# High weights against both parts of an activation in one 512-column matmul

## The chip, the core and the metric

The kernel runs on one core of one Trainium2 chip. The metric is device time in microseconds, the median of three timed runs. TensorE (PE in the profile) does the matmuls, with its weight loads listed apart as PEld; VectorE is DVE, ScalarE is ACT, GpSimd is POOL and SyncE is SP, which here issues the weight transfers.

## What is computed

Five blocks follow one another on 256 tokens (272 in the first part, with 16 meta tokens ahead) of 2048 features, all in float32:

```python
h = h + mla_mixer(rms_norm(h))        # 272 tokens
h = h + swiglu(rms_norm(h))           # first feed-forward, 272 tokens
h = h + rglru_mixer(rms_norm(h))      # recurrent mixer
h = h + swiglu(rms_norm(h))           # second feed-forward
h = rms_norm(h)[:, N_META:]           # 256 tokens
for layer in range(2):                # second block: four attentions, gate, output projection
    x = x + einsum(y * silu(gate), w_out[layer])

def swiglu(h, w_gu, w_down):
    g, u = split(h @ w_gu, 2)
    return (silu(g) * u) @ w_down     # 2048 -> 2 x 5632 -> 2048

def rglru_mixer(h, w_in, ...):
    xb, yb = split(h @ w_in, 2)       # 2048 -> 2 x 2048
    yb = gelu(yb)
    xb = conv(xb); r, i = gates(xb)   # two 128x128 gate matrices for each of 16 blocks
    hs = scan(a(r), b(i, xb))
    return (hs * yb) @ w_o
```

## The kernel before

Features lie on the 128 partitions and tokens on the free axis, so a gemm makes one tile of 128 output features by 256 or 272 tokens. Every float32 number is split into a high and a low part of type float32r, `xh` and `xl` for an activation, `wh` and `wl` for a weight, and a product is three matmuls for each 128 features of the contraction (`mm3`, L224 to L226): `wh` with `xh`, `wh` with `xl`, `wl` with `xh`. All three add into the same PSUM tile `p`. A first or second feed-forward `gu` gemm has 16 such steps, a `dn` (down) gemm 11, an `lru_in` gemm 16 and an `lru_o` gemm 8.

Weights come from HBM in pieces of up to 1024 columns (`wblock`): SP loads `wraw` (4 buffers), ACT casts it into `wh` (L212, 6 buffers), DVE subtracts into `wl` (L187, 5 buffers). There are four PSUM tiles `p`.

The feed-forward (`ffn`) has four chunks of 11 hidden tiles. For each hidden tile f, `gu` runs two gemms (gate and up), DVE multiplies each by the norm's factor (L478, L480), ACT takes silu, DVE multiplies, and the product is split (`hid`). Then 16 `dn` gemms, one for each tile m of h, are added to h by DVE (L497). One hidden tile of the next chunk is made ahead of the `dn` gemms, except in the last chunk. In the last chunk of the second feed-forward, each finished tile of h goes through the final norm's tile work: squares on ACT and POOL, a scale on DVE (L936), and a split (L251, L252).

The recurrent mixer (`lru`) goes over 16 blocks n, in groups of four. Each has a 272-column gemm for `xb`, a convolution on DVE (L524), a split `xch`, `xcl`, two gates `pg` (three matmuls each), and a 256-column gemm for `yb`. After four blocks the scan is done on DVE (L570). Then two passes of 16 gemms over `lru_o`, added to h by DVE (L582).

The second block (`block2`) runs 32 rounds of a pair of heads with gemms of q, k and gate, attention, and output projections.

The order in which each engine takes its instructions is set at build time by a scheduler that orders the traced program by its own estimate of times. A tile has to wait until a buffer of its pool is free. Before, the high and low parts are separate slots of the pool `s` of 66; the small pools `a`, `w`, `r`, `b` hold 10, 11, 3 and 5.

Of the kernel before, what the change touches and what calls it, by code (L numbers as in the profile page):

```python
# [9 lines left out]
F32 = mybir.dt.float32  # L10
# [5 lines left out]
D = 2048  # L16
# [27 lines left out]

SLOTS = {"s": 66, "a": 10, "w": 11, "r": 3, "b": 5}
WB = (4, 6, 5)
# [13 lines left out]


class Lazy:
    """Traced at its first use, so that it queues behind what is traced before."""

# [10 lines left out]
class Net:  # L75
# [48 lines left out]
    def use_log_exp(self, after=None):  # L124
        """One table set for exp and ln; the next logarithm is queued behind its load."""
        if after is None:
            self.log_exp = self.nc.scalar.preload_act_table_set("natural_log_exp_and_others")
        else:
            with self.tc.issue_after(after.ins):
                self.log_exp = self.nc.scalar.preload_act_table_set("natural_log_exp_and_others")  # L130
# [14 lines left out]
    def zeropad(self, n):  # L145
        """Pairs of [128, 256] operands whose first half stays zero."""
        self.zp = []
        self.zpi = 0
        for _ in range(n):
            pr = (self.slot("zph", F32R), self.slot("zpl", F32R))  # L150
            for t in pr:
                self.nc.gpsimd.memset(t[:, 0:128].bitcast(F32), 0.0)
            self.zp.append(pr)

    def split_zp(self, x):
        """split(x) into columns 128..255 of a zero-padded pair."""
        h, l = self.zp[self.zpi % len(self.zp)]
        self.zpi += 1
        self.nc.scalar.copy(h[:, 128:256], x)
        self.sub(l[:, 128:256], x, h[:, 128:256])  # L160
        return h, l

    def stackpad(self, n):
        """Tiles of three bands of 16 rows, with zeros between them."""
        self.st3 = [self.slot("st3", F32R) for _ in range(n)]
        self.st3i = 0
        for t in self.st3:
            self.nc.gpsimd.memset(t[0:96].bitcast(F32), 0.0)

    def stack3(self, x, n, order):  # L170
        """High, high and low part of 16 rows (by order: high first, low last) as bands of one contraction."""
        t = self.st3[self.st3i % len(self.st3)]
        self.st3i += 1
        b = [t[32 * i:32 * i + 16, 0:n] for i in order]
        self.nc.scalar.copy(b[0], x)
        self.nc.scalar.copy(b[1], x)
        self.sub(b[2], x, b[0])
        return t
# [9 lines left out]

    def split(self, x, name, n, p=slice(0, 128), tag="s"):
        nc = self.nc  # L190
        h = self.slot(name + "h", F32R, tag=tag)
        l = self.slot(name + "l", F32R, tag=tag)
        nc.scalar.copy(h[p, 0:n], x)
        self.sub(l[p, 0:n], x, h[p, 0:n])
        return h, l
# [6 lines left out]
    def wblock(self, ap, n, wp=1024, raws=None):  # L202
        """Loads n columns in pieces of wp and splits each into its two float32r parts."""
        nc = self.nc
# [23 lines left out]
    def gemm(self, p, w, xs, sl, off=0):  # L228
        n = len(xs)
        for k, (xh, xl) in enumerate(xs):  # L230
            self.mm3(p, self.wcol(w, off + k * 128, 128), (xh[:, sl], xl[:, sl]), k == 0, k == n - 1)

    def rsqrt(self, name, ms, n, scale=1.0, eps=EPS):
        """scale / sqrt(ms + eps): exp(-ln/2) and one Newton step."""
        nc = self.nc
# [10 lines left out]
    def norm_tile(self, st, m, src, gcol, sl, n, sq=True):  # L246
        """One feature tile on its way into a norm: split(src*g) and the running sum of squares."""
        nc = self.nc
        xh = self.slot("xh", F32R)
        xl = self.slot("xl", F32R)  # L250
        self.last_norm = nc.scalar.activation(xh[:, 0:n], src, AF.Copy, scale=gcol)  # L251
        nc.vector.scalar_tensor_tensor(xl[:, 0:n], src, gcol, xh[:, 0:n].bitcast(F32), ALU.mult, ALU.subtract)  # L252
        st.setdefault("x", []).append((xh, xl))
        if sq:
            self.sumsq(st, src, n)
# [20 lines left out]

# [1 line left out]
    def mla(self, st, nxt):  # L278
# [13 lines left out]
        for i in (4, 5, 6, 7, 0, 1, 2, 3, 8):  # L292
# [9 lines left out]
            if i == 5:  # L302
                with self.tc.issue_after(self.last_norm.ins):
# [7 lines left out]
                    st["accs"] = [sq[0][:, j * T:j * T + T] for j in range(4)]  # L311
                c = self.slot("craw")
                nc.vector.tensor_tensor(c, p4, rb(), ALU.mult)
                self.sumsq(skv_st, c, T)
                ckv_raw.append(c)
            c = self.slot("craw")
            nc.vector.tensor_tensor(c, p, rb(), ALU.mult)
# [72 lines left out]
    def split_stacked(self, x, name, n):  # L390
        """Of each half (one head) of x, both parts in one tile: the high one in its own half, the low one in the other."""
        out = []
# [19 lines left out]
    def softmax(self, s, n, rows, mask):  # L412
        """exp(s + mask - max) / sum over the free axis; kept negated up to the exponential."""
        nc = self.nc
# [44 lines left out]

# [1 line left out]
    def ffn(self, l, st, t0, after):  # L461
        """after(m): what follows on the finished tile m of h."""
        nc, a = self.nc, self.a
# [6 lines left out]
        def gu(f):  # L470
            w = self.wblock(a[f"gu{l}"][f], 2048)
            pg = self.ps()[:, 0:n]
            self.gemm(pg, w, X, sl)
            w = self.wblock(a[f"gu{l}"][FF + f], 2048)
            pu = self.ps()[:, 0:n]
            self.gemm(pu, w, X, sl)
            g = self.tmp("g")[:, sl]
# [8 lines left out]
        for c in range(C):  # L486
# [5 lines left out]
            for m in range(KD):  # L492
                w = self.wblock(a[f"dn{l}"][c, m], FCH * 128)
                p = self.ps()[:, 0:n]
                self.gemm(p, w, H[c * FCH:(c + 1) * FCH], sl)
                hm = self.h[m][:, t0:T]
                nc.vector.tensor_tensor(hm, hm, p, ALU.add)  # L497
                if c == C - 1:
                    after(m)

# [1 line left out]
    def lru(self, st, nxt):  # L502
# [7 lines left out]
        for n0 in range(0, KD, 4):  # L510
            la, th = self.big("la"), self.big("th")
            IX, YB = [], []
            for i in range(4):
# [31 lines left out]
                w = self.wblock(a["lru_in"][16 + n], 2048)  # L545
                p = self.ps()[:, 0:SEQ]
                self.gemm(p, w, X, slice(NM, T))
                if i % 2 == 0:
# [25 lines left out]
        for c in range(2):  # L574
            for mb in range(8):
                w = self.wblock(a["lru_o"][c, mb], 2048)
                for m2 in range(2):
                    m = mb * 2 + m2
                    p = self.ps()[:, 0:SEQ]
                    self.gemm(p, w, Y[c * 8:c * 8 + 8], sl, m2 * 1024)  # L580
                    hm = self.h[m][:, NM:T]
                    nc.vector.tensor_tensor(hm, hm, p, ALU.add)  # L582
                    if c == 1:
                        self.norm_tile(nxt, m, hm, self.col("norm_ffn1", m), sl, SEQ)

    def lru_coef(self):
        """-8*softplus(-lambda) on [128, 16]."""
        nc = self.nc
# [17 lines left out]

# [1 line left out]
    def block2(self, l, st, rb, first_done, after):  # L608
# [6 lines left out]
        def forget(ft):  # L615
            """Running sum of softplus(-(f + bias)) as one row per head."""
            p = self.psh.tile([128, 512], F32, tag="h", name="fT")
# [15 lines left out]
        def values(mx, hf):  # L633
# [5 lines left out]
            for tt in range(2):  # L639
# [8 lines left out]
                p = p[:, sl]  # L648
                vh = self.slot("vh", F32R)[:, sl]
                vl = self.slot("vl", F32R)[:, sl]  # L650
                rc = rcol()[:, tt:tt + 1]
# [78 lines left out]
    def softplus(self, z, rows, n, tag="w"):  # L730
        """max(z, 0) + log(1 + exp(-|z|))"""
        nc = self.nc
# [46 lines left out]
    def diagpad(self, n):  # L779
        """Pairs of [128, 256] operands, zero off the two diagonal blocks (one per head)."""  # L780
        self.dp = []
        self.dpi = 0
        for _ in range(n):
            pr = (self.slot("dph", F32R), self.slot("dpl", F32R))
            for t in pr:
# [4 lines left out]
    def diag(self, x, c):  # L790
        """The two heads of x (its columns c) as the blocks of a diagonal pair."""
        pr = self.dp[self.dpi % len(self.dp)]
# [7 lines left out]
    def soft(self, q, k, masks, NC, i):  # L800
        """Transposed weights of a pair of heads: of keys 0..127, and of keys 128..255 for queries 128..255."""
        nc = self.nc
# [93 lines left out]
    def rcols(self, rb):  # L896
        """Per-token factors as columns: the diagonal blocks of the broadcast rows."""
        nc = self.nc
# [7 lines left out]

# [1 line left out]
    def all(self):  # L908
# [19 lines left out]
    def second(self, st):  # L928
# [13 lines left out]
        def factors():  # L942
            """The two norms in a row: 1 / sqrt(ms + eps), and 1 / sqrt(ms2 / (ms + eps) + eps) times it."""
            ms, ms2 = self.pa("ms")[:, sl], self.pa("ms2")[:, sl]
# [29 lines left out]

# [1 line left out]
def _tiles(w):  # L976
    """[K, M] -> [M/128, 128 (k), K/128 * 128 (m)]"""
    k, m = w.shape
# [4 lines left out]
def _cols(v):  # L983
    """[n*128] -> [128, n]"""
    return np.asarray(v).reshape(-1, 128).T
# [43 lines left out]
def _arrays(inp):  # L1029
# [48 lines left out]
    def kchunks(w, kc, mpb):  # L1078
        """[K, D] -> [K/(kc*128), D/(128*mpb), 128, mpb*kc*128]"""
        k, d = w.shape  # L1080
# [38 lines left out]
```

## Time and profile before

| what | us |
|---|---|
| median of 3 runs (3217.25 to 3219.3) | 3217.95 |
| span of the profiled execution | 3216.7 |
| PE busy | 3187.9 |
| DVE busy | 2162.1 |
| ACT busy | 1755.1 |
| POOL busy | 606.6 |

The span runs from the first to the last instruction of one profiled execution; it lies 1.25 us under the median. Busy times overlap between engines. A matmul's own duration (some 280 ns for 256 columns) contains the time through the pipeline, so what a matmul costs in a stream is the distance from its start to the start of the next one.

### The profile page before, as it was taken

How to read it: one execution, taken by the hardware profiler on the slowest of the kernel's cores; microseconds unless marked ns; L12 is line 12 of the kernel's file. 1: busy time of each engine (PE TensorE's matmuls, PEld its weight loads, DVE VectorE, ACT ScalarE, POOL GpSimd, SP SyncE). 2: the span in 40 equal slices, each digit the busy share in tenths (PEclk: the TensorE clock that was granted, in tenths of full speed). 3: DMA queues.
4: the chain of work that ended last, by engine and by line, in shares of the span. 5: the costliest groups of instructions: out<-in, count | busy, mean ns of one | idle time of the engine just before them, and what ended most of it. 6: DMA issues, size and time to landing. Idle time of an engine off the chain costs nothing.

```text
span 3216.7 us, 64486 instructions
## 1 busy us (share of the span) xinstructions
PE 3187.9 (99%) x25996; PEld 3154.1 (98%) x25996; DVE 2162.1 (67%) x3672; ACT 1755.1 (55%) x2971; POOL 606.6 (19%) x743
## 2 busy tenths in 40 slices
PE   8999999999999999999999999999999999999999
PEld 8998999999999999999999999999999999999999
DVE  7777655555555678865555555568788778778876
ACT  6655533434444576754444444456677666667764
POOL 2000100000000134310000000023244463144453
PEclk9999999999999999999999999999999999999999
DMA  6343556556565555566565656656555545555554
GB/s 215 113 122 111 173 165 187 176 160 190 161 193 173 165 185 175 161 194 186 169 202 172 202 180 186 190 166 200 165 166 170 169 151 174 158 174 168 170 161 131
DMA packets 164862, 549.43 MB, mean 171 GB/s; under 512 B 18753, under 2 KB 37441, under 8 KB 164561
## 3 DMA queue, kind: packets, MB, share of 16 engines
q1 hardware_dynamic: 162720, 540.49, 54.5%
q0 software_dynamic: 1840, 4.82, 0.5%
q8 instruction: 203, 3.33, 0.4%
q14 instruction: 99, 0.80, 0.1%
HBM read 543.13 MB, written 2.10 MB: 170 GB/s over the span
## 4 chain that ended last, share of the span: by engine, by line
PE 92%; DVE 3%; ACT 2%; issue 2%; POOL 1%; DMA 0%; SPq 0%; POOLq 0%; DVEq 0%; ACTq 0%
PE p L224 29%; PE p L225 29%; PE p L226 29%; DVE wl L187 1%; ACT wh L212 1%; PE o L225 1%; PE o L224 0%; PE o L226 0%; DVE xl L252 0%; PE s L224 0%; PE s L225 0%; PE s L226 0%; PE s L438 0%; DVE hs L570 0%; POOL gwl L531 0%
## 5 line engine op out<-in xcount | busy, mean ns | idle before, releaser
L212 ACT CAST wh<-wraw 128x1024 fp32r<-128x1024 f32 (+2 forms) x1108 | 1086.8, 982 | 1003.4 <-PE p L225 777.9
L187 DVE TENSOR_TENSOR wl<-wraw,wh 128x1024 fp32r<-128x1024 f32 (+2 forms) x1108 | 1293.2, 1168 | 334.0 <-issue 248.9
L224 PE MATMUL p<-xh,wh 128*128 128x256 f32 (+1 forms) x5104 | 1451.9, 284 | 7.9 <-ACT wh L212 6.7
L225 PE MATMUL p<-xl,wh 128*128 128x256 f32 (+1 forms) x5104 | 1452.1, 285 | 1.0 <-DVE xl L252 1.0
L226 PE MATMUL p<-xh,wl 128*128 128x256 f32 (+1 forms) x5104 | 1450.1, 284 | 0.3 <-DVE wl L187 0.2
L224 PEld LDWEIGHTS p<-xh,wh 128*128 128x128 f32 x5104 | 963.6, 189 | 10.4 <-ACT wh L212 6.7
L225 PEld LDWEIGHTS p<-xl,wh 128*128 128x128 f32 x5104 | 963.6, 189 | 5.0 <-DVE xl L252 2.4
L226 PEld LDWEIGHTS p<-xh,wl 128*128 128x128 f32 x5104 | 963.3, 189 | 1.9 <-DVE wl L187 1.0
L225 PE MATMUL p<-hidl,wh 128*128 128x272 f32 (+1 forms) x1408 | 400.2, 284 | 0.0
L226 PE MATMUL p<-hidh,wl 128*128 128x272 f32 (+1 forms) x1408 | 400.1, 284 | 0.0
L224 PE MATMUL p<-hidh,wh 128*128 128x272 f32 (+1 forms) x1408 | 399.9, 284 | 0.0
L226 PEld LDWEIGHTS p<-hidh,wl 128*128 128x128 f32 x1408 | 265.2, 188 | 0.0
L225 PEld LDWEIGHTS p<-hidl,wh 128*128 128x128 f32 x1408 | 265.1, 188 | 0.0
L224 PEld LDWEIGHTS p<-hidh,wh 128*128 128x128 f32 x1408 | 265.1, 188 | 0.0
L265 POOL TENSOR_TENSOR acc<-acc,sq 128x256 f32<-128x256 f32 (+1 forms) x81 | 76.3, 942 | 989.8 <-ACT sq L264 909.1
L224 PE MATMUL p<-yh,wh 128*128 128x256 f32 x768 | 216.6, 283 | 0.0
L225 PE MATMUL p<-yl,wh 128*128 128x256 f32 x768 | 216.0, 282 | 0.0
L226 PE MATMUL p<-yh,wl 128*128 128x256 f32 x768 | 215.9, 281 | 0.0
L265 POOL TENSOR_TENSOR accf<-accf,sq 128x256 f32<-128x256 f32 x15 | 15.4, 1026 | 706.2 <-ACT sq L264 706.2
L225 PEld LDWEIGHTS p<-yl,wh 128*128 128x128 f32 x768 | 145.0, 189 | 0.6 <-issue 0.5
L224 PEld LDWEIGHTS p<-yh,wh 128*128 128x128 f32 x768 | 144.6, 189 | 0.9 <-DVE h L704 0.5
L226 PEld LDWEIGHTS p<-yh,wl 128*128 128x128 f32 x768 | 145.0, 189 | 0.1
(352 smaller groups left out, 4269.5 us busy)
## 6 DMA issues: line engine op xcount, KB each, us to landing
wraw<-gu SPq DMA_DIRECT2D x352, 512.0 KB, 4.3
wraw<-dn SPq DMA_DIRECT2D x128, 512.0 KB, 3.5
wraw<-in SPq DMA_DIRECT2D x128, 512.0 KB, 4.3
wraw<-lru_in SPq DMA_DIRECT2D x64, 512.0 KB, 4.1
wraw<-g SPq DMA_DIRECT2D x64, 512.0 KB, 3.8
wraw<-out SPq DMA_DIRECT2D x64, 512.0 KB, 3.7
wraw<-v SPq DMA_DIRECT2D x56, 512.0 KB, 4.1
wraw<-dn SPq DMA_DIRECT2D x128, 192.0 KB, 2.6
```

Of the source, the lines that this page charges most:

```text
L187: return self.nc.vector.tensor_tensor(out, x, h.bitcast(F32), ALU.subtract)
L212: nc.scalar.copy(h[:, 0:c], raw)
L224: nc.tensor.matmul(p, lh, rh, start=first, stop=False)
L225: nc.tensor.matmul(p, lh, rl, start=False, stop=False)
L226: nc.tensor.matmul(p, ll, rh, start=False, stop=last)
L265: (eng or nc.gpsimd).tensor_tensor(st[key], st[key], s[:, 0:n], ALU.add)
```

## The change

For gemms of 256 tokens in the second feed-forward (`gu` and `dn`) and in the recurrent mixer (the `yb` half of `lru_in`, and `lru_o`), the three matmuls of a contraction step become two (`gemm2`): `wh` against `xh` and `xl` side by side, 512 columns into the two halves of a PSUM tile, and `wl` against `xh`, 256 columns into the first half. So the two halves of the PSUM tile have to be added. Where the gemm ends in a residual add (`gemm_add`), DVE adds the halves to h one after the other. Elsewhere (`gemm_any`) ACT copies the second half into a tile `sum`, and DVE adds the first half to it; what follows then reads `sum` in place of `p`. For 272 tokens nothing changes in the matmuls, since two parts would be 544 columns.

To stand side by side, the two parts of an activation are now one tile `Pair` of 2 x 272 columns. They have a pool `x` of 27 pairs, and the pool `s` of single tiles falls from 66 to 12. The tile `craw` of the first mixer moves to the pool `b`. All splits use the pairs, in the parts of the kernel whose matmuls stay the same too.

```diff
-SLOTS = {"s": 66, "a": 10, "w": 11, "r": 3, "b": 5}
+SLOTS = {"x": 27, "s": 12, "a": 10, "w": 11, "r": 3, "b": 5}
...
+    def pair(self, name, n=T):
+        t = self.slots["x"].tile([128, 2 * T], F32R, tag="x", name=name)
+        p = Pair((t[:, 0:n], t[:, T:T + n]))
+        p.both = t.rearrange("p (j c) -> p j c", c=T)[:, :, 0:n]
+        return p
...
+    def gemm2(self, p, w, xs, sl, off=0):
+
+        n = len(xs)
+        for k, x in enumerate(xs):
+            wh, wl = self.wcol(w, off + k * 128, 128)
+            self.nc.tensor.matmul(halves(p, SEQ), wh, x.both[:, :, sl], start=k == 0, stop=False)
+            self.nc.tensor.matmul(p[:, 0:SEQ], wl, x[0][:, sl], start=False, stop=k == n - 1)
+
+    def gemm_any(self, w, xs, sl, off=0):
+
+        p = self.ps()
+        n = sl.stop - sl.start
+        if n > SEQ:
+            p = p[:, 0:n]
+            self.gemm(p, w, xs, sl, off)
+            return p
+        self.gemm2(p, w, xs, sl, off)
+        t = self.tmp("sum")[:, 0:SEQ]
+        self.nc.scalar.copy(t, p[:, SEQ:512])
+        self.nc.vector.tensor_tensor(t, p[:, 0:SEQ], t, ALU.add)
+        return t
+
+    def gemm_add(self, hm, w, xs, sl, off=0):
+
+        p = self.ps()
+        n = sl.stop - sl.start
+        if n > SEQ:
+            self.gemm(p[:, 0:n], w, xs, sl, off)
+            self.nc.vector.tensor_tensor(hm, hm, p[:, 0:n], ALU.add)
+            return
+        self.gemm2(p, w, xs, sl, off)
+        for j in range(2):
+            self.nc.vector.tensor_tensor(hm, hm, p[:, j * SEQ:j * SEQ + SEQ], ALU.add)
...
             w = self.wblock(a[f"gu{l}"][f], 2048)
-            pg = self.ps()[:, 0:n]
-            self.gemm(pg, w, X, sl)
+            pg = self.gemm_any(w, X, sl)
...
                 w = self.wblock(a[f"dn{l}"][c, m], FCH * 128)
-                p = self.ps()[:, 0:n]
-                self.gemm(p, w, H[c * FCH:(c + 1) * FCH], sl)
-                hm = self.h[m][:, t0:T]
-                nc.vector.tensor_tensor(hm, hm, p, ALU.add)
+                self.gemm_add(self.h[m][:, t0:T], w, H[c * FCH:(c + 1) * FCH], sl)
...
-                p = self.ps()[:, 0:SEQ]
-                self.gemm(p, w, X, slice(NM, T))
+                p = self.gemm_any(w, X, slice(NM, T))
...
-                    p = self.ps()[:, 0:SEQ]
-                    self.gemm(p, w, Y[c * 8:c * 8 + 8], sl, m2 * 1024)
                     hm = self.h[m][:, NM:T]
-                    nc.vector.tensor_tensor(hm, hm, p, ALU.add)
+                    self.gemm_add(hm, w, Y[c * 8:c * 8 + 8], sl, m2 * 1024)
```

**On PE, in a `gu` gemm of the second feed-forward.** Two contraction steps of one gemm before (out<-moving,weights and the moving columns):

```order
L224 MATMUL p_25154<-xh_16911,wh_25144 128x256
L225 MATMUL p_25154<-xl_16912,wh_25144 128x256
L226 MATMUL p_25154<-xh_16911,wl_25145 128x256
L224 MATMUL p_25154<-xh_16956,wh_25144 128x256
L225 MATMUL p_25154<-xl_16957,wh_25144 128x256
```

and three steps of such a gemm with the change:

```order
L255 MATMUL p_22954<-x_16411,wh_22944 128x512
L256 MATMUL p_22954<-x_16411,wl_22945 128x256
L255 MATMUL p_22954<-x_16448,wh_22944 128x512
L256 MATMUL p_22954<-x_16448,wl_22945 128x256
L255 MATMUL p_22954<-x_16473,wh_22944 128x512
```

Nothing moved between the steps; L224 and L225 became one instruction.

**On DVE, in the last chunk of the second feed-forward**, one period between two `dn` gemms before, where `h` is the residual and `p` the gemm's PSUM tile:

```order
L497 TENSOR_TENSOR h_93<-h_93,p_26128 128x256
L187 TENSOR_TENSOR wl_26293<-wraw_26290,wh_26292 128x1024
L936 TENSOR_SCALAR h_93<-h_93,cols_83 128x256
L252 SCALAR_TENSOR_TENSOR xl_26168<-h_93,cols_83,xh_26167 128x256
L187 TENSOR_TENSOR wl_26299<-wraw_26296,wh_26298 128x384
L497 TENSOR_TENSOR h_93<-h_93,p_26186 128x256
```

and with the change:

```order
L282 TENSOR_TENSOR h_93<-h_93,p_23737 128x256
L193 TENSOR_TENSOR wl_23869<-wraw_23866,wh_23868 128x1024
L303 SCALAR_TENSOR_TENSOR x_23672<-h_93,cols_83,x_23672 128x256
L282 TENSOR_TENSOR h_93<-h_93,p_23737 128x256
L978 TENSOR_SCALAR h_93<-h_93,cols_83 128x256
L193 TENSOR_TENSOR wl_23875<-wraw_23872,wh_23874 128x384
L282 TENSOR_TENSOR h_93<-h_93,p_23784 128x256
```

The second add stands four places behind the first, and the subtraction for the norm (L252, now L303) now belongs to the tile before and has moved ahead of the scale (L936, now L978).

**On ACT, in the recurrent mixer**, at the last block of a group of four, before (`gate` reads a gate's PSUM tile `pg`; `gel` is the gelu of `yb`):

```order
L212 CAST wh_14419<-wraw_14417 128x1024
L553 ACTIVATE gel_14195<-yb_14032 128x256
L556 ACTIVATE gel_14195<-gel_14195 128x256
L538 ACTIVATE gate_14122<-pg_14118,cols_83 128x272
L538 ACTIVATE gate_14128<-pg_14124,cols_83 128x272
L212 CAST wh_14506<-wraw_14504 128x1024
L544 ACTIVATE th_13513<-la_13512 128x272
```

and with the change:

```order
L229 CAST wh_14294<-wraw_14292 128x1024
L584 ACTIVATE gate_13934<-pg_13930,cols_83 128x272
L268 COPY sum_13990<-p_13957 128x256
L584 ACTIVATE gate_13940<-pg_13936,cols_83 128x272
L590 ACTIVATE th_13364<-la_13363 128x272
L229 CAST wh_14343<-wraw_14341 128x1024
```

The copy of the `yb` gemm's second half stands between the two gates, and the gelu of that block has moved behind them.

## Rows read from the trace of the kernel before

**Rows 1.** The page, its first part: busy us, share of span, instructions.

```profile
PE 3187.9 (99%) x25996; PEld 3154.1 (98%) x25996; DVE 2162.1 (67%) x3672; ACT 1755.1 (55%) x2971; POOL 606.6 (19%) x743
```

**Rows 2.** The page, the chain that ended last, by engine.

```profile
PE 92%; DVE 3%; ACT 2%; issue 2%; POOL 1%; DMA 0%; SPq 0%; POOLq 0%; DVEq 0%; ACTq 0%
```

**Rows 3.** Windows, inside both feed-forwards: stretch, its us, busy us per engine.

```profile
core 0: us, PE busy (x) PEld busy (x) DVE busy (x) ACT busy (x) POOL busy (x), PEclk, DMA share, GB/s
350.00:1130.00 780.00, 780.00 (x6229) 780.00 (x6228) 421.93 (x552) 325.12 (x417) 10.31 (x13) 1.00 0.58 175
1450.00:2180.00 730.00, 730.00 (x6170) 730.00 (x6169) 416.47 (x557) 322.05 (x425) 26.48 (x25) 1.00 0.60 184
```

**Rows 4.** Timeline of PE, second block: first and last of 32 pairs of 512 columns.

```profile
2241.06 0.40 PE L225 MATMUL o<-p,vh 128*128 128x512 f32 x1
2241.30 0.40 PE L226 MATMUL o<-p,vl 128*128 128x512 f32 x1
2241.53 0.28 PE L224 MATMUL o<-p,vh 128*128 128x256 f32 x1
...
3190.71 0.39 PE L225 MATMUL o<-p,vh 128*128 128x512 f32 x1
3190.94 0.39 PE L226 MATMUL o<-p,vl 128*128 128x512 f32 x1
3191.17 0.28 PE L224 MATMUL o<-p,vh 128*128 128x256 f32 x1
```

**Rows 5.** Timeline of PE, second block: L817's moving operand is two separate pieces.

```profile
2571.03 0.27 PE L817 MATMUL s<-nb,one 8*128 8x256 f32 x1
2571.14 0.43 PE L818 MATMUL s<-nb,one 8*128 8x512 f32 x1
```

**Rows 6.** Groups by line and form, DVE and ACT, window 1450 to 2180.

```profile
L187 DVE TENSOR_TENSOR wl<-wraw,wh 128x1024 fp32r<-128x1024 f32 x231 | 283.2, 1226 | 65.8 <-issue 54.3 <-PE p L226 7.6 <-ACT wh L212 2.1
...
L497 DVE TENSOR_TENSOR h<-h,p 128x256 f32<-128x256 f32 x62 | 26.0, 419 | 21.9 <-PE p L226 21.9
L478 DVE TENSOR_TENSOR g<-p,rsr 128x256 f32<-128x256 f32 x43 | 18.2, 424 | 72.5 <-PE p L226 72.5
...
L212 ACT CAST wh<-wraw 128x1024 fp32r<-128x1024 f32 x232 | 243.8, 1051 | 323.9 <-PE p L225 259.5 <-issue 49.1 <-DMA wraw<-gu 11.1
...
L193 ACT CAST hidh<-u 128x256 fp32r<-128x256 f32 x43 | 17.5, 406 | 45.3 <-DVE u L482 45.3
```

**Rows 7.** Timeline of DVE, one period of the last chunk.

```profile
2152.22 0.55 DVE L187 TENSOR_TENSOR wl<-wraw,wh 128x384 fp32r<-128x384 f32 x1
2152.69 0.41 DVE L497 TENSOR_TENSOR h<-h,p 128x256 f32<-128x256 f32 x1
2153.07 1.40 DVE L187 TENSOR_TENSOR wl<-wraw,wh 128x1024 fp32r<-128x1024 f32 x1
2154.39 0.82 DVE L936 TENSOR_SCALAR h<-h,cols 128x256 f32<-128x256 f32 x1
2155.80 0.49 DVE L252 SCALAR_TENSOR_TENSOR xl<-h,cols,xh 128x256 fp32r<-128x256 f32 x1 [0.58 <-ACT xh L251]
2156.20 0.55 DVE L187 TENSOR_TENSOR wl<-wraw,wh 128x384 fp32r<-128x384 f32 x1
```

**Rows 8.** Waits of PE in the recurrent mixer, 1130 to 1450: us, times, longest.

```profile
PE pg L224 <- ACT xch L193: 7.0, 5, 1.9
```

**Rows 9.** Windows: end of a mixer group, and the whole second block.

```profile
1250.00:1280.00 30.00, 28.18 (x218) 27.96 (x217) 26.45 (x40) 20.10 (x35) 14.15 (x16) 0.94 0.52 164
2182.00:3217.00 1035.00, 1026.56 (x8499) 1014.49 (x8497) 811.98 (x1587) 676.13 (x1332) 425.26 (x538) 1.00 0.53 165
```

More of the change, by code (lines that the diff above doesn't have):

```diff
@@ L59, in block @@
     return [t[:, j * 128:j * 128 + 128] for t in pair]
+class Pair(tuple):
+    both = None
 class Lazy:
@@ L149, in zeropad @@
         for _ in range(n):
-            pr = (self.slot("zph", F32R), self.slot("zpl", F32R))
+            pr = self.pair("zp")
             for t in pr:
@@ L187, in sub, with split @@
         return self.nc.vector.tensor_tensor(out, x, h.bitcast(F32), ALU.subtract)
-    def split(self, x, name, n, p=slice(0, 128), tag="s"):
-        nc = self.nc
+    def pair(self, name, n=T):
[3 more added lines that the diff above has]
+        return p
+    def split(self, x, name, n, p=slice(0, 128), tag="x"):
+        nc = self.nc
+        if tag == "x":
+            pr = self.pair(name, n)
+            nc.scalar.copy(pr[0][p], x)
+            self.sub(pr[1][p], x, pr[0][p])
+            return pr
         h = self.slot(name + "h", F32R, tag=tag)
@@ L248, in norm_tile @@
         nc = self.nc
-        xh = self.slot("xh", F32R)
-        xl = self.slot("xl", F32R)
+        pr = self.pair("x", n)
+        xh, xl = pr
         self.last_norm = nc.scalar.activation(xh[:, 0:n], src, AF.Copy, scale=gcol)
         nc.vector.scalar_tensor_tensor(xl[:, 0:n], src, gcol, xh[:, 0:n].bitcast(F32), ALU.mult, ALU.subtract)
-        st.setdefault("x", []).append((xh, xl))
+        st.setdefault("x", []).append(pr)
         if sq:
@@ L311, in mla @@
                     st["accs"] = [sq[0][:, j * T:j * T + T] for j in range(4)]
-                c = self.slot("craw")
+                c = self.slot("craw", F32, [128, 512], "b")[:, 0:T]
                 nc.vector.tensor_tensor(c, p4, rb(), ALU.mult)
@@ L315, in mla @@
                 ckv_raw.append(c)
-            c = self.slot("craw")
+            c = self.slot("craw", F32, [128, 512], "b")[:, 0:T]
             nc.vector.tensor_tensor(c, p, rb(), ALU.mult)
@@ L471, in gu @@
             w = self.wblock(a[f"gu{l}"][f], 2048)
-            pg = self.ps()[:, 0:n]
-            self.gemm(pg, w, X, sl)
+            pg = self.gemm_any(w, X, sl)
             w = self.wblock(a[f"gu{l}"][FF + f], 2048)
-            pu = self.ps()[:, 0:n]
-            self.gemm(pu, w, X, sl)
+            pu = self.gemm_any(w, X, sl)
             g = self.tmp("g")[:, sl]
@@ L648, in values @@
                 p = p[:, sl]
-                vh = self.slot("vh", F32R)[:, sl]
-                vl = self.slot("vl", F32R)[:, sl]
+                vh, vl = self.pair("v", n)
                 rc = rcol()[:, tt:tt + 1]
@@ L783, in diagpad @@
         for _ in range(n):
-            pr = (self.slot("dph", F32R), self.slot("dpl", F32R))
+            pr = self.pair("dp")
             for t in pr:
```

## The prediction

> **What bounds the kernel now.** I read the shares of busy time first. PE is busy 99% of the span and DVE 67%, so only DVE could come near PE [rows 1]. Then I read the chain of work that ended last: 92% of it is PE [rows 2]. So the time is the sum of PE's matmuls, and a change counts by what it does to their spacing and to the few places where PE waits. Third come windows inside the two feed-forwards, since a matmul's own duration does not tell its spacing. In the first one, with 272 columns, 6229 matmuls fill 780 us, 125.2 ns each. In the second, with 256 columns, 6170 fill 730 us, 118.3 ns each [rows 3]. PE never idles in either. DVE is busy 57% of the second window (416 of 730) and ACT 44%, and the DMA engines 60%.
>
> **What the change removes.** Each changed contraction step has two instructions in place of three, with the same 768 columns. So nothing of the arithmetic goes; what goes is one start of a matmul and one load of `wh`. I count the steps: the second feed-forward has 88 `gu` gemms of 16 and 64 `dn` gemms of 11, which is 1408 + 704; the mixer has 16 `yb` gemms of 16 and 32 `lru_o` gemms of 8, which is 256 + 256. That is 2624 steps.
>
> The price of a step now is 3 x 118.3 = 354.9 ns. With the change it is one matmul of 512 columns and one of 256. The trace has the first kind: the attentions of the second block run 32 pairs of 512-column matmuls back to back, each with other weights. From the start of the first to the start of what follows the second, the first pair takes 0.47 us and the last 0.46 us; the mean over the 32 pairs, from the first to the last of these rows, is 0.463 us, or 232 ns for one [rows 4]. Two matmuls of 256 columns are 236.6 ns. So a step costs 232 + 118.3 = 350.3 ns and saves 4.6 ns, and the sum is 2624 x 4.6 = 12.1 us.
>
> The bounds of this price are wide. Upwards: if all that a 256-column matmul takes beyond its columns were paid for each start, it could be read from the two widths. They differ by 6.9 ns in 16 columns, 0.43 ns each; 256 x 0.43 is 110.4 ns, which leaves 7.9 ns a start, and 2624 x 7.9 = 20.7 us. Downwards: by the first pair alone a 512-column matmul is 235 ns, which saves 1.6 ns a step or 4.2 us. I take 232 because it is the operation itself, in a stream and with a fresh load of weights each time.
>
> The Trainium skill (TensorE: Matmul & The Clock Gate, section Back-to-back issue gap) gives the distance between warm matmuls as columns over 2.4 GHz plus about 2.5 ns. By it a step would save 2.5 ns and the kernel an estimated 6.6 us. Neither 118.3 nor 232 ns agrees with the formula (109.2 and 215.8 ns), and the measured spacing decides.
>
> Does it matter that the moving operand now lies in two pieces (256 columns, a gap of 16, 256 columns)? L817 reads two pieces of 128 columns; where it follows a matmul of as few rows, the next one starts 0.11 us later [rows 5]. A plain 256-column matmul takes 0.118. So I add nothing.
>
> **What the change adds.** DVE gets one instruction for each changed gemm, 88 + 64 + 16 + 32 = 200 by 0.42 us, or 84 us in all; ACT gets a copy for 104 of them by 0.41 us, 43 us [rows 6]. I cost these at nothing in the second feed-forward, because PE's matmuls hide them. A hidden tile takes PE 2 x 16 x 350.3 ns = 11.2 us. In it DVE has four subtractions of some 1.23 us and, with the two sums, six pieces of 0.42 us, or 7.4 us. ACT has four casts of 1.05 and four pieces of 0.41, or 5.8 us. What waits behind a `sum` on DVE is the next subtraction into `wl`; the order puts four of those ahead of it, two gemms of PE's work, so a late `sum` does not reach PE. The PSUM tile is held longer by a copy and an add, under 1 us, with four tiles and 5.6 us a gemm.
>
> At one place the cover is thin: the last chunk of the second feed-forward. There DVE has a period of 3.98 us for each tile m, of which 0.58 is a wait for ACT [rows 7], while PE needs 33 x 118.3 = 3.90 us for the gemm. With the change DVE has one more add of 0.38 (start to start in these rows), and the order puts the split of the tile before in place of the tile just scaled, so the wait can go: 3.98 - 0.58 + 0.38 = 3.78 us, against 11 x 350.3 = 3.85 us on PE. It fits by 0.07 us. If the wait stayed, DVE would need 4.36 us, and 16 tiles would be 8 us late, less what four PSUM tiles and the `wl` split ahead absorb. I charge nothing.
>
> The other place is the recurrent mixer. PE waits 7.0 us there, five times, for `xch` of the block whose gates are next [rows 8], and DVE is busy 26.45 of the 30 us around the end of a group [rows 9]. The copy of the second half now stands on ACT between two gates, and the sum stands on DVE ahead of the multiplication that starts the next block's chain. If all of this (0.41 + 0.38 us) went into each of the five waits, it would be 4.0 us; if PE's other gemms hid it, nothing. I take 2.5 us.
>
> **What the change moves.** Pools. In the feed-forwards 16 pairs of the input and 11 of the hidden tiles fill the 27 pairs, so the split of the hidden tile made ahead waits for the last `dn` gemm of a chunk. On ACT the casts of two gemms (11 us of PE) stand ahead of it, and what is queued behind it is 2.1 us of casts for the third gemm; nobody on PE waits. The order of SP's weight loads is the same as before. In the second block seven pairs are left beside the input and the padded operands; before it was some 17 single slots (66 less 32 of the input, 8 of the padded operands and 9 of constants). PE idles there 8.4 of 1035 us now [rows 9]; I charge nothing and keep it as a rival.
>
> **Sum.** Against the profiled span: 3216.7 - 12.1 + 2.5 = 3207.1. The median of the runs lies 1.25 us above that span, so the runs should show 3208.3; I say 3208.
>
> **The rivals.**
> - *A start costs more than I think, and more is saved.* At 7.9 ns a start the gain is 20.7 us: 3217.95 - 20.7 + 2.5 = 3200. For it speaks the step from 256 to 272 columns [rows 3]; against it, the 512-column pairs themselves [rows 4].
> - *Nearly all of the spacing goes with the columns.* At 235 ns the gain is 4.2 us, and with the mixer's 2.5 us the kernel comes to 3216, no change that counts. For it speaks the first pair of rows 4. The rule of the skill cited above ends near here: by its 6.6 us the estimate would be 3214.
> - *The smaller pool makes the second block wait: slower.* That block has 32 rounds of a pair of heads. A round holds two pairs of values and two of q and k, so of seven pairs three are left for the next round, and its second split would wait until the attention before has read its q or k. PE would then lack work. It decides from (12.1 - 2.5) / 32 = 0.3 us a round; at 0.75 us a round it is 24 us, and 3208 + 24 = 3232. Against it: before, 17 slots were little more, and PE waited for named reasons only a few times; for it: DVE is busy 812 of 1035 us there [rows 9], so a split that is freed late also queues.
>
> **How the numbers follow.** My forecast, 3203 to 3212, has a chance of 0.5; the larger gain 0.13; the small one 0.22; the slower one 0.15. The predicted time is that of the likeliest, 3208. The range runs from 3195 (the larger gain, and the mixer's waits no longer) to 3225; above it lies about half of the slower rival, 0.08, and below it 0.05. A measurement of this kernel tells about 0.2%, 6.4 us, from no change, so faster means under 3211.5: most of the forecast (0.43) and all of the larger gain (0.13) make 0.56. Within 0.2% lie the small gain, the rest of the forecast and a little of the slower case, 0.32. Slower is 0.12.
>
> **What would show it.** In the window of the second feed-forward the changed steps should come every 350 ns, 343 to 347 if the first rival holds, and 353 if the second does; its whole stretch should be about 9.7 us shorter (2112 x 4.6). PE should show no wait there. The mixer should show waits for `xch` of 7 to 11 us. In the last chunk DVE's period should be under 3.9 us. In the second block PE's idle time should stay near 8 us; 20 us or more would mean the pool. I am wrong if 512 columns read from two pieces cost more than 232 ns, or if the order, which the scheduler made anew for all parts of the kernel, puts waits where there were none.

## The result, and the profile after

The changed kernel takes 3237.3 us, the median of 5 runs (3236.1 to 3238.2), against 3218.6 for the kernel before (5 runs beside it). The ratio is 1.0059, with a 95% interval from 1.0048 to 1.0070: slower by 0.6%, where 3208 was forecast, and above the upper end of the forecast range, 3225.

The first part of the page answers to [rows 1]: PE is as busy as before with 2624 instructions fewer, and DVE has 98 us more.

```profile
PE 3188.3 (99%) x23372; PEld 3038.8 (94%) x23372; DVE 2260.1 (70%) x3872; ACT 1782.8 (55%) x3072; POOL 615.3 (19%) x743
```

So the page alone doesn't tell where the time went. I cut the span at matmuls that both programs have, by their starts in PE's timeline: the first that reads `hid` (it follows the first mixer and the first `gu` gemms), the first into `pg` (in the recurrent mixer), the first that reads `y`, the product that `lru_o` takes in (`lru_o` begins), the last that reads `hid` (end of the second feed-forward), and the last of all.

| stretch | before | after | difference |
|---|---|---|---|
| start to first `hid` | 482.7 | 486.4 | +3.7 |
| to first `pg` | 668.7 | 667.7 | -1.0 |
| to first `y`: mixer | 189.8 | 208.7 | +18.9 |
| to last `hid`: `lru_o`, second feed-forward | 841.5 | 829.2 | -12.3 |
| to the last matmul: second block | 1029.9 | 1040.3 | +10.4 |

The gain is there, in its place, and three other stretches lose more than it. The windows show the same (the columns are those of [rows 3]; the third last number is PEclk, PE's granted clock as a share of full speed): the mixer, the inside of the second feed-forward, and the second block.

```profile
1130.00:1345.00 215.00, 195.01 (x1307) 182.31 (x1306) 162.55 (x235) 139.13 (x226) 67.50 (x81) 0.95 0.48 164
1450.00:2180.00 730.00, 730.00 (x4176) 638.52 (x4175) 479.69 (x716) 353.42 (x520) 28.00 (x28) 1.00 0.57 187
2192.00:3232.30 1040.30, 1032.18 (x8491) 1018.44 (x8490) 825.11 (x1587) 675.54 (x1331) 428.35 (x533) 1.00 0.48 163
```

In the second row 4176 matmuls are 2088 steps in 730 us, 349.6 ns a step, and PE has no idle time. In the first, PE is idle for 20 of 215 us. The waits of PE over the whole span (us in total, times, longest) name what for:

```profile
PE pg L241 <- ACT xch L210: 15.9, 3, 7.3
PE p L241 <- ACT wh L229: 9.8, 2, 6.8
PE hms L805 <- POOL qsql L802: 5.0, 6, 1.8
PE p L255 <- DVE sum L269: 4.1, 3, 2.2
...
PE ms L322 <- POOL acc L316: 1.6, 1, 1.6
```

The first answers to [rows 8]: 15.9 us in three long waits where there were 7.0 in five short ones. Of the 9.8 us for `wh`, 6.8 are one wait at the start, which the kernel before has too. The wait for `sum` is new. Of the kernel before:

```profile
PE p L224 <- ACT wh L212: 6.7, 1, 6.7
PE hms L763 <- POOL qsql L760: 2.3, 2, 1.1
```

**One of the mixer's stalls.** PE's timeline at the end of a group of four blocks (start, duration, and in brackets the wait ahead; `...` marks rows left out):

```profile
1272.49 0.29 PE L243 MATMUL p<-x,wl 128*128 128x272 f32 x1
1280.08 0.82 PE L241 MATMUL pg<-xch,gwh 128*128 128x272 f32 x2 [7.30 <-ACT xch L210]
...
1281.41 0.43 PE L243 MATMUL pg<-xch,gwl 128*128 128x272 f32 x1
1282.78 0.76 PE L255 MATMUL p<-x,wh 128*128 128x512 f32 x1 [0.94 <-DVE sum L269]
...
1283.55 0.63 PE L255 MATMUL p<-x,wh 128*128 128x512 f32 x1
1283.98 0.41 PE L256 MATMUL p<-x,wl 128*128 128x256 f32 x1
1284.19 0.63 PE L255 MATMUL p<-x,wh 128*128 128x512 f32 x1
```

Three things stand here one behind the other. PE has run out of gemms and waits 7.3 us for the `xch` of the next group. Then it waits for `sum`, since all four PSUM tiles are held. ACT's timeline shows why that one is late too: its copy stands in line behind a gate, which needs the matmuls that PE has just been able to start. The table load ahead of that gate ends at 1281.33, about with these matmuls; both kernels have four such loads of 1.28 us at the mixer's gates, and no run takes their part out.

```profile
1279.61 0.42 ACT L210 CAST xch<-xc 128x272 fp32r<-128x272 f32 x1 [2.61 <-DVE xc L570]
1280.05 1.28 ACT L584 ACT_TABLE_LOAD   x1
1281.42 0.49 ACT L584 ACTIVATE gate<-pg,cols 128x272 f32<-128x272 f32 x1
1281.80 0.36 ACT L268 COPY sum<-p 128x256 f32<-128x256 f32 x1
```

Third, the steps then come every 0.64 us (1283.55 to 1284.19) in place of 0.35: the granted clock has fallen. Here are two windows behind two of the stalls:

```profile
1222.00:1226.00 4.00, 4.00 (x13) 3.42 (x14) 3.12 (x5) 0.97 (x2) 2.13 (x4) 0.50 0.24 91
1283.00:1287.00 4.00, 4.00 (x13) 3.42 (x14) 3.16 (x6) 1.80 (x5) 2.44 (x5) 0.50 0.12 37
```

PEclk is 0.50 in both, which is 1.2 GHz, after the idle 7.3 us in the second case and after two waits of 2.6 and 2.2 us (at 1218.28 and 1221.86) in the first. The kernel before has one such place in its mixer, behind a wait of 1.8 us (0.57 from 1264 to 1268); the changed kernel has three. I summed what the distances between matmul starts in the mixer have beyond the normal ones (118.3, 125.2 and 232 ns): gaps of over 0.4 us grew from 7.8 to 21.4 us, and lengthened steps from 2.5 to 7.3. Together that is +18.4 us of the mixer's 18.9.

### The profile page after: what moved, and what is told of

Read it like the earlier page. It is cut to its first block, busy times and chain, and to the rows that moved or that the text cites. A ratio compares the mean times of both kernels' runs of the same rounds, so it can differ in the third digit from the quotient of the medians.

```text
span 3236.5 us, 59492 instructions
## 1 busy us (share of the span) xinstructions
PE 3188.3 (99%) x23372; PEld 3038.8 (94%) x23372; DVE 2260.1 (70%) x3872; ACT 1782.8 (55%) x3072; POOL 615.3 (19%) x743
## 5 line engine op out<-in xcount | busy, mean ns | idle before, releaser
L241 PE MATMUL p<-x,wh 128*128 128x272 f32 (+1 forms) x3440 | 987.1, 287 | 11.0 <-ACT wh L229 9.8
L243 PE MATMUL p<-x,wl 128*128 128x272 f32 (+1 forms) x3440 | 986.2, 287 | 1.4 <-DVE wl L193 1.4
L242 PE MATMUL p<-x,wh 128*128 128x272 f32 (+1 forms) x3440 | 983.3, 286 | 0.0
L241 PEld LDWEIGHTS p<-x,wh 128*128 128x128 f32 x3440 | 650.6, 189 | 15.0 <-ACT wh L229 10.0
L242 PEld LDWEIGHTS p<-x,wh 128*128 128x128 f32 x3440 | 651.9, 190 | 1.8 <-DVE x L303 0.5
L243 PEld LDWEIGHTS p<-x,wl 128*128 128x128 f32 x3440 | 651.0, 189 | 2.6 <-DVE wl L193 1.8
L255 PE MATMUL p<-x,wh 128*128 128x512 f32 x1664 | 589.3, 397 | 4.1 <-DVE sum L269 4.1
L256 PE MATMUL p<-x,wl 128*128 128x256 f32 x1664 | 468.8, 282 | 0.0
L255 PEld LDWEIGHTS p<-x,wh 128*128 128x128 f32 x1664 | 315.2, 189 | 77.6 <-issue 2.5
L256 PEld LDWEIGHTS p<-x,wl 128*128 128x128 f32 x1664 | 316.1, 190 | 0.0
L255 PE MATMUL p<-hid,wh 128*128 128x512 f32 x704 | 246.2, 394 | 0.0
L243 PE MATMUL p<-hid,wl 128*128 128x272 f32 x704 | 202.8, 288 | 0.0
L241 PE MATMUL p<-hid,wh 128*128 128x272 f32 x704 | 202.7, 288 | 0.0
L242 PE MATMUL p<-hid,wh 128*128 128x272 f32 x704 | 202.5, 288 | 0.0
L256 PE MATMUL p<-hid,wl 128*128 128x256 f32 x704 | 197.1, 280 | 0.0
```

Source lines behind the costliest of these rows:

```text
L241: nc.tensor.matmul(p, lh, rh, start=first, stop=False)
L242: nc.tensor.matmul(p, lh, rl, start=False, stop=False)
L243: nc.tensor.matmul(p, ll, rh, start=False, stop=last)
L255: self.nc.tensor.matmul(halves(p, SEQ), wh, x.both[:, :, sl], start=k == 0, stop=False)
L256: self.nc.tensor.matmul(p[:, 0:SEQ], wl, x[0][:, sl], start=False, stop=k == n - 1)
```

## Experiments

**Pools alone, and the gemm of `yb` alone.** The first run keeps the pools and the pairs and does every gemm in three matmuls (one line, in `gemm_any` and in `gemm_add`); the second is the changed kernel with only `yb` in its old form.

```diff
-        if n > SEQ:
+        if n > 0:
```

> The pools of pairs (27 and 12) and the tile craw in pool b stay as in the change; every gemm goes back to three matmuls and one reader of its PSUM tile. Theory: the change lost in two places of unlike cause, the mixer (about 19 us, from the yb gemm's new form) and start plus second block (about 14 us, from the pools). Then this kernel keeps the 14 us and neither the 12 us gain nor the mixer's loss: 3231 us, PE waits for xch about 7 us. Rival: the pools cost nothing and all comes from the new gemms and their order: 3218 us.

```diff
-                p = self.gemm_any(w, X, slice(NM, T))
+                p = self.ps()[:, 0:SEQ]
+                self.gemm(p, w, X, slice(NM, T))
```

> Only the yb gemm of the mixer goes back to three matmuls read by one DVE multiplication; the feed-forward and the mixer's output gemms keep the new form. Theory: the yb form costs the mixer its PE work at the end of a group; PE's wait for xch falls from 15.9 to about 7 us and the time to 3237 - 17 = 3220 us. Rival: the mixer waits because 16 pairs of input and 12 of output do not fit in 27: wait stays near 16 us, time near 3237 us.

They took 3234.8 us (ratio 1.0052, 1.0037 to 1.0067) and 3219.1 (1.0003, 0.9994 to 1.0012). So the sum has three terms: the pools cost 17.1 us, the 512-column matmuls outside `yb` save 15.7, and `yb` costs 18.2. Nearly all of the 15.7 lie in the stretch from the first `y` to the last `hid`, which is 843.6 us with the pairs alone and 829.2 with these matmuls. The second run's mixer is back at 189.6 us, with the waits of before:

```profile
PE pg L241 <- ACT xch L210: 6.8, 5, 1.9
```

### The mixer

**The halves of `yb` without the copy on ACT.** DVE multiplies each half by the norm's factor and POOL adds them.

```diff
-                nc.vector.tensor_tensor(yb, p, rb()[:, NM:T], ALU.mult)
+                y2 = self.tmp("sum")[:, 0:SEQ]
+                nc.vector.tensor_tensor(yb, p[:, 0:SEQ], rb()[:, NM:T], ALU.mult)
+                nc.vector.tensor_tensor(y2, p[:, SEQ:512], rb()[:, NM:T], ALU.mult)
+                nc.gpsimd.tensor_tensor(yb, yb, y2, ALU.add)
```

> The yb gemm keeps its 512-column form, but no copy on ACT: DVE multiplies each half by the norm factor and POOL adds them. Theory a: the PSUM tile is held because the copy stands on ACT behind a gate that itself waits; without the copy the waits for xch and for sum go, time about 3222 us. Theory b: what matters is how much PE work the scheduler puts between the last gates of a group and the first of the next (23 us before, 16 to 22 with the change, 17 to 22 here), and the chain needs about 24 us whoever reads PSUM; waits for xch stay above 12 us, time 3233 us or more.

3229.4 us (1.0035, 1.0022 to 1.0048), the mixer 200.2. The time lies between the two that I had expected, 3222 and 3233, so either theory tells a part. The waits for `sum` are nearly gone, those for `xch` are not:

```profile
PE pg L241 <- ACT xch L210: 14.7, 3, 6.8
PE p L255 <- DVE sum L599: 0.8, 1, 0.8
```

**The copy without the new matmuls.** `yb` in three matmuls, with a copy on ACT and one more instruction on DVE that leaves the number as it is.

```diff
+                t = self.tmp("sum")[:, 0:SEQ]
+                nc.scalar.copy(t, p)
+                nc.vector.tensor_tensor(t, p, t, ALU.max)
+                p = t
```

> The version with the yb gemm in its old form (3219.1), but its one half is copied by ACT into a tile sum and DVE takes the larger of the two, which is the same number: the two added instructions without the new matmuls. The order has 23.7, 17.8 and 21.6 us of gemms at the ends of the groups. If the added step on ACT and DVE is the cause (by the scheduler's order or by itself), the mixer lasts 195 to 206 us and the time is 3225 to 3236. If the 512-column matmuls of yb themselves were the cause, it stays at 190 us and 3219.

3237.4 us (1.0059, 1.0046 to 1.0073), 1.4 us over the range of the first theory; the mixer, 205.2, is inside its range. The two added instructions alone lose in all what the change loses, so the wide matmuls of `yb` are not needed for the loss. Against the version with `yb` in its old form, 15.6 us lie in the mixer and 4.0 behind it, where an early gemm of `lru_o` waits for a `sum` too (2.1 us):

```profile
PE pg L241 <- ACT xch L210: 10.0, 3, 6.6
PE p L241 <- DVE sum L596: 6.2, 3, 3.1
PE p L255 <- DVE sum L596: 2.1, 1, 2.1
```

**PE's order.** Between the last gates of a group and the first of the next, the scheduler puts 23.3, 23.1 and 23.1 us of gemms before the change and 21.9, 16.2 and 18.4 after it (matmuls in its order times their spacing): it lets PE do the next gemms ahead of the last gates (at the second group 11.4 us of gemms stand ahead of them in the trace, where there were 6.7). The chain that ends in the next `xch` (gates, scan, and ahead of them the last blocks' work on DVE) takes 23 to 24 us at such a place in both (from the last gate's matmul to `xch`: before 1237.7 to 1262.1, after 1256.5 to 1279.6). This run holds two gemms back:

```diff
-                self.gemm(p, w, X, full)
+                with self.tc.issue_after(hold.ins) if hold and i == 1 else ExitStack():
+                    self.gemm(p, w, X, full)
...
-                p = self.gemm_any(w, X, slice(NM, T))
+                with self.tc.issue_after(hold.ins) if hold and i == 0 else ExitStack():
+                    p = self.gemm_any(w, X, slice(NM, T))
```

where `hold` is the last gate matmul of the group before.

> The changed kernel (3237.3) with one addition in the mixer: the next two gemms of PE (yb of the next group's first block, xb of its second) may not start before the gates of a group's last block. The order then puts 22.7, 22.5 and 22.1 us of gemms between the last gates of a group and the first of the next (21.9, 16.2 and 18.4 in the changed kernel, 23.3, 23.1, 23.1 before). If the order of PE's work is what lengthened the mixer, it comes back to 190 to 195 us from 208.8, the waits for xch to 6 to 9 us, and the time is 3219 to 3224. If it is the copy on ACT, behind the gate and with the PSUM tile held, the mixer stays at 200 us or more and the time at 3229 or more, as in the run in which DVE takes both halves.

3232.6 us (1.0046, 1.0030 to 1.0061), the mixer 204.6: both as I had expected if the copy was the cause. The waits for `xch` fell as the theory of the order wants, and the waits for `sum` took part of their place:

```profile
PE pg L241 <- ACT xch L210: 8.5, 4, 3.7
PE p L255 <- DVE sum L269: 7.3, 3, 2.9
```

And the two longest waits for `xch` stand elsewhere: not at the next group's first gates but ahead of a group's own last gates (the other is 3.68 us, at 1311.31). There the held gemms had stood; in the trace 4.4 us of gemms are left ahead of these gates, where the changed kernel has 11.4.

```profile
1251.39 0.82 PE L241 MATMUL pg<-xch,gwh 128*128 128x272 f32 x2 [3.73 <-ACT xch L210]
```

So neither theory was enough alone, and the numbers of the order's theory were missed by 9 us. Both together:

> The hold of PE's gemms (3232.6 by itself) together with yb's halves taken by DVE and added by POOL, without the copy on ACT (3229.4 by itself). The order now puts 23.1, 17.7 and 22.5 us of gemms at the ends of the groups. If the mixer's loss has these two parts, the order and the PSUM tile held by the copy, both waits shrink together: for sum under 1.5 us (7.3 with the hold alone), for xch 7 to 11 us with one long one, where 17.7 stands (14.7 with the halves on DVE alone); the mixer lasts 193 to 199 us and the time is 3221 to 3226. If the second instruction for yb's halves, wherever it stands, is what delays the chain, the mixer stays at 200 us or more and the time at 3228 or more.

3224.2 us (1.0023, 1.0013 to 1.0032), the mixer 193.8:

```profile
PE pg L241 <- ACT xch L210: 8.7, 5, 3.7
PE p L255 <- DVE sum L604: 2.4, 3, 1.3
```

The mixer gives back 14.9 of its 18.9 us, where the single edits gave 8.5 and 4.1. So the removal of the copy (with it the add goes from DVE to POOL) is worth 8.5 us without the hold and 10.8 with it, the hold 4.1 with the copy and 6.4 without: the copy is the larger part. The wait for `sum` is 0.9 us longer than I expected. Of the 4 us that the mixer still lacks, the trace shows a wait of 3.72 us for `xch` ahead of the second group's last gates (1246.28), the place that the hold had emptied in the run before; no run tests that cause.

### The pools

**One pair more, two single slots more.** 28 pairs in the changed kernel; and 14 single slots in the version with `yb` in its old form.

```diff
-SLOTS = {"x": 27, "s": 12, "a": 10, "w": 11, "r": 3, "b": 5}
+SLOTS = {"x": 28, "s": 12, "a": 10, "w": 11, "r": 3, "b": 5}
```

> One pair more (28 in place of 27), all else as in the change. If a full pool of pairs is what makes start and second block wait, one pair more gives back a good part of their 14 us: 3228 us or less. If the single slots (12) or the order as such are the cause: 3237 us, as with 27.

> The version with only the yb gemm in its old form (3219.1), with 14 single slots in place of 12 beside the 27 pairs. If the single slots are what the second block lacks, it gets back half or more of its 10 us: 3209 to 3214, the landmark from the last hid to the end 1033 to 1036 us. If the pairs as tiles are the cause, or the order of the scheduler, 3217 to 3221 and 1039 to 1041 us.

3238.2 us (1.0063, 1.0046 to 1.0080) and 3219.9 (1.0002, 0.9993 to 1.0012): neither size gives anything back.

**High and low apart again.** All gemms in three matmuls, `pair` returns two tiles, out of 54 single slots beside the 12, or out of one pool of 66.

```diff
-        t = self.slots["x"].tile([128, 2 * T], F32R, tag="x", name=name)
+        return Pair(self.slots["x"].tile([128, T], F32R, tag="x", name=name + k)[:, 0:n] for k in "hl")
```

> Pools alone (every gemm of three matmuls, as in the run of the pairs alone, 3234.8), but the high and the low part are two tiles again, out of a pool of 54 single slots; the split into 54 + 12 slots stays. If the loss comes from the part of the memory that the second block's constants and gates can use (12 single slots), nothing changes: 3232 to 3237, the second block 9 to 11 us longer than before. If it comes from the pair as one tile (both halves are freed and waited for together, and the scheduler orders by that), the time goes back to that of before: 3217 to 3221, the start and the second block as before.

> As the run with 54 + 12 single slots, but one pool of 66 for all, as in the kernel before; only craw lies in the pool b. Every theory of the pools expects the time of before here, 3217 to 3221. If it is slower by 5 us or more, it is craw or the order that the scheduler happens to find, and not the pools.

3221.1 us (1.0011, 1.0001 to 1.0020) and 3217.3 (0.9996, 0.9987 to 1.0005). One pool of separate tiles takes as long as the kernel before. The divided pool costs some 3 us: 6.0 more in the second block, where I had expected none, and about 2 less in the stretches ahead of it. The pair as one tile is the other 14 of the 17.

**What the pair does at the start** stands in the changed kernel's timeline of ACT:

```profile
17.53 4.10 ACT L358 ACTIVATE sq<-h 128x1088 f32<-128x1088 f32 x4
21.53 3.88 ACT L229 CAST wh<-wraw 128x1024 fp32r<-128x1024 f32 x4
```

and in that of PE, which waits for the first of these casts:

```profile
22.62 0.39 PE L241 MATMUL p<-x,wh 128*128 128x272 f32 x1 [2.99 <-ACT wh L229]
```

The scheduler put four squares ahead of the second gemm's weight casts; before, two casts came first (16.4 and 17.7), and the squares at 19.1. This run puts them back, in the version with `yb` in its old form (`last_cast` is the last weight cast traced so far):

```diff
-                with self.tc.issue_after(self.last_norm.ins):
+                with self.tc.issue_after(self.last_cast.ins):
```

> The version with only the yb gemm in its old form (3219.1); in the first mixer the four squares of h on ACT are put behind the weight casts of the second gemm, as the order of before had them. If that order is what the start lost (PE waited for wh at 19 and 23 us), the first hid comes 3 us earlier, near 483, and the time is 3216. If the start is late for another reason, it stays at 3219. The second block should stay as it was, 1040 us.

3214.4 us (0.9985, 0.9976 to 0.9995); the first `hid` comes at 480.2 us, 5.7 earlier, where I had expected 3.

**What it does at the second block.** POOL's timeline in the changed kernel, where the second of its layers begins: 13 memsets of the padded pairs stand ahead of the last add into `acc`.

```profile
2716.43 3.03 POOL L829 MEMSET dp<- 64x128 f32 x13
2719.55 1.80 POOL L316 TENSOR_TENSOR acc<-acc,sq 128x256 f32<-128x256 f32 x1
```

PE's timeline behind it:

```profile
2721.40 0.70 PE L322 MATMUL ms<-acc,ones 128*128 128x256 f32 x2 [1.60 <-POOL acc L316]
```

Two more runs put the memsets behind the add, and then also move `qsql` (the low part of the squares of q and k), for which PE waits 5.0 us there, from POOL to DVE:

```diff
+                  with self.tc.issue_after(self.last_acc.ins):
...
-        nc.gpsimd.tensor_tensor(vl, v, vh.bitcast(F32), ALU.subtract)
+        nc.vector.tensor_tensor(vl, v, vh.bitcast(F32), ALU.subtract)
```

> The version with yb in its old form and the squares behind the casts (3214.4), and POOL's memsets of the padded pairs dp put behind the last add into acc at the start of each layer of the second block. If the waits of PE for acc (1.6 and 1.4 us) come from the memsets ahead of that add, they go, and the time is 3211 to 3212.5. If the add is late for another reason, 3214 to 3215.

> The version with yb in its old form and both orders at the starts put right (3211.3), with the subtraction qsql of the second block on DVE in place of POOL. If POOL's order (padded operands, gates and rope ahead of qsql) is what still makes the second block wait, the 4.5 us of waits of hms go, its stretch falls from 1036.4 to 1031 to 1034 us, and the time is 3206 to 3209. If the products are late for another reason (the cast on ACT, or the scheduler fills PE less), the waits for hms stay, only with DVE as the releaser, and the time is 3210 to 3214.

3211.3 us (0.9979, 0.9970 to 0.9988) and 3207.6 (0.9967, 0.9955 to 0.9979), the second block 1036.4 and 1032.8 us. The longest waits that PE has left from the end of the second feed-forward on, in the last of them:

```profile
PE s L241 <- POOL dp L841: 0.7, 2, 0.4
PE p L241 <- DVE h L747: 0.5, 1, 0.5
```

**The same three edits on the kernel before**, and on the whole change with the mixer's gemms held:

> The kernel before, with the same three edits as the best version (squares of h behind the casts, memsets behind the last add into acc, qsql on DVE) and nothing of the change. If these edits only mend what the new pools broke, it stays at 3216 to 3220. If they help the old kernel as much as the new one, it comes to 3207 to 3211, and the best version's gain is theirs and not that of the 512-column matmuls. By its waits (2.3 us for qsql, about 1 for accf, a start that is 2.5 us later than the best version's) it should lie between, at 3212 to 3216.

> All of the change, yb too, with the three orders put right: the mixer's gemms held back as in the run before, the squares of h behind the casts, the memsets behind the last add. If the order is all that the mixer lost, it saves the 1.2 us of yb's 256 steps besides: 3210 to 3213, at or under the version with yb in its old form. If the copy on ACT costs by itself, 3215 to 3222.

The kernel before stays at 3218.0 us (1.0001, 0.9992 to 1.0010); I had thought that it would gain some microseconds. So the edits mend what the pairs broke, and the 10.6 us by which 3207.6 beats the kernel before beside it (3218.2) come in the main from the 512-column matmuls. In the profiled executions their stretch is 12.3 us shorter and the second block 2.9 longer; the way to the first `pg` is some 2 shorter, of which the edits give the kernel before 1.2. The whole change, with two of the edits (`qsql` left on POOL) and the copy on ACT kept, takes 3226.0 (1.0026, 1.0017 to 1.0036), 4 us over the upper of my two ranges, for the reason that the held run gave.

## Why the prediction was wrong

- **The price of a step** was right: 349.6 ns against 350.3. The stretch with 2368 of the 2624 steps is 12.3 us shorter, where 2368 x 4.6 is 10.9. The rivals at 347 and 353 ns a step fall. That the saving came so close has some luck in it, for the old step is not the same in all versions: 700 us inside the second feed-forward (1450 to 2150) hold 5916 matmuls of 256 columns in the kernel before, 5903 with the pairs alone and 5936 in the one pool of 66, or 118.3, 118.6 and 117.9 ns each. Three of these less 349.6 are 4.1 to 6.2 ns. The Trainium skill's rule for the gap of an isolated matmul (TensorE: Matmul & The Clock Gate, section Back-to-back issue gap) would by an estimate save 5.9 us in this stretch; the trace doesn't agree.
- **DVE and ACT in the second feed-forward** were rightly costed at nothing: PE is busy 730.00 of 730 us. In the last chunk DVE scales a tile every 3.51 us on the mean, (2197.6 - 2145.0) / 15, under the 3.9 foretold:

```profile
L978 DVE TENSOR_SCALAR h<-h,cols x16: 340/498/839, 2145.0 to 2197.6; 128x256 f32<-128x256 f32 x16
```

- **The mixer is the first step that failed**, with its term of 2.5 us. "If all of this (0.41 + 0.38 us) went into each of the five waits, it would be 4.0 us" bounded the added instructions by their own length. They cost 20 us, the 18.9 and yb's gain of 1.2. The copy alone, with the old matmuls, costs nearly as much: the order gives PE less to do during the chain of 23 to 24 us, and the copy, queued on ACT behind a gate, keeps the PSUM tile and makes a second wait; lengthened steps, nearly all behind the stalls at the lower clock, add 4.8 us. I had quoted ACT's rows with the copy between the gates and had not asked which tile it holds meanwhile, nor counted the gemms that PE's order has left at a group's end.
- **The pools are the second**, a term put at nothing. "I charge nothing" cost 17 us. The rival that I kept for it had the right sign and place and mostly the wrong mechanism: more slots give nothing, and pairs instead of separate tiles cost 14 of the 17 us, at the start too, which I hadn't looked at. That its 3232 came near the measured 3237.3 is luck: it had 24 us in the second block, which lost 10.4, and the mixer made up the rest. Where the mechanism is shown, it is the order that the scheduler makes of other tiles: squares ahead of casts, memsets ahead of an add. My sentence that the order "puts waits where there were none" was on the list of what would make me wrong, without a price.
- The idle time in the second block, which was to stay near 8 us, is not a good measure: by busy time it is 8.1 us in 1040.30 after and 4.3 in the same stretch before, a third of the 10.4 us. The sign that I had named for the pool, 20 us or more, stayed away although the pools cost.

What stays open: whether the hold makes the wait that the mixer still has, why the scheduler orders pairs otherwise, and why the second block of the best version (3207.6 us) is still 2.9 us longer than before.

## What to carry to other kernels

When a scheduler makes the order anew, an instruction added off the critical path is not bounded by its own length: count the work that the order leaves for the waiting engine beside each long chain, before and after, and ask which buffer each added reader holds while it stands in line. When two buffers become one, look at the order in parts of the kernel whose arithmetic stays the same, first where an engine starts up or changes phase. Take the pieces apart early: here the part that was meant to gain did so, and two runs showed that it was the other two parts that lost.

## What the runs showed that I had not expected

- After a stall of 7.3 us in the mixer PE was granted half its clock for some 7 us (0.50 from 1280 to 1286, 0.62 from 1286 to 1288), so that a wait cost more than its length: 4.8 us of lengthened steps on top of 13.6 us of longer gaps.
- Matmuls whose moving operand `x` lies in a pair came a little slower in the second block: 118.4 ns from start to start on the mean over some 5600 of them in the versions of 3211.3 and 3207.6 us, against 117.8 in the kernel before and 117.9 in that with 54 single slots. That is 0.5 to 0.6 ns each, some 3 us, about what the best version's second block still lacks. But the pair as such does not explain it: in the second feed-forward the kernel before, with separate tiles, has 118.5 ns on such matmuls (some 4070 of them, 1450 to 2150), and the one with 54 single slots 117.9. No run here tells whether it is the place in memory or something else.
